# FFN input products of an encoder block: four instead of three of eight K-tile pairs by Strassen's scheme, with part of the sums formed by an accumulating DMA

## The chip, the cores and the metric

One core of one Trainium2 chip runs the whole block as one program. The metric is the device time of one execution in microseconds (us). TensorE (PE) multiplies, VectorE (DVE) and ScalarE (ACT) work elementwise, GpSimd (POOL) and SyncE (SP) here mostly issue DMAs; each engine takes its instructions in order from a queue of its own.

## The reference, cut to what matters

One layer, 256 tokens of width 2048, float32: a first FFN, a mixer of two attentions, a cross attention, a second FFN. The change lies in the two FFNs alone (`D_FF` is 5504):

```
def swiglu_ffn(x, w_in, w_out):
    g, u = jnp.split(x @ w_in, 2, axis=-1)
    return (jax.nn.silu(g) * u) @ w_out
h = layer_norm(ALPHA * h + 0.5 * swiglu_ffn(h, ffn1_w_in, ffn1_w_out), ...)
...
h = layer_norm(ALPHA * h + 0.5 * swiglu_ffn(h, ffn2_w_in, ffn2_w_out), ...)
```

## The kernel before

**Split products.** Each float32 operand is split into `hi` (a cast on ACT) and `lo = value - hi` (a subtraction on DVE); a product is three matmuls: hi·hi, lo·hi, hi·lo. All weights are streamed once, mostly 1 MB at a time, by SP into one of three `raw` buffers, then split into units of 128x1024 (four `hi` and four `lo` buffers).

**FFN input.** The 5504 columns of gate and of up are done in groups `j` of 512 columns (`j` = 0 to 9, and a narrow group 10). In a group the K dimension (2048) is walked in eight *items*, each a pair of K tiles (1 MB of weights: for each of the two K tiles, 512 columns of up and 512 of gate). An item done plainly (`mm_pair`, L296) is 2 K tiles x 2 token halves x 2 (gate, up) x 3 = 24 matmuls into four PSUM tiles. Group 0 is built apart in each FFN (`start`, `first_group`); groups 1 to 9 of both FFNs, 18 in all, go through `in_group`.

**Strassen items.** A pair of K tiles, two token halves and two column blocks is a 2x2 by 2x2 block product. For the items in `SUMS_AT` = (2, 4, 6) it is done with seven block products (`mm_sums`, L340), 7 x 3 = 21 matmuls. This needs sums of weight blocks. `form_sums` makes them on DVE in the buffer t (tag H5): one add of 1024 columns and two of 512 (L183). The two halves of t are then split (ACT L244, DVE L245) into two blocks, called here A (read by matmuls 10 to 15 of the item) and B (by matmuls 16 to 21); their buffers rotate over the tags X2, X3 and H4. It also needs sums of x, the forms (`sum_forms`, L311 and L315), made once per FFN for each of the Strassen items. After the last Strassen item of a group, `shared` combines four more PSUM tiles (L569 to L574) and `hidden` adds them and applies SiLU (L616 to L619).

**Turn and output.** The product of a group is transposed on PE eight times (L631) and split into H0 to H3: the *turn*, which is woven into the work after it, ahead of item 2 of the next group. After 12, then 16, then 15 K tiles (`F_SPLIT`) the output product (`out_proj`, L285) runs over what has been turned; there the last turn stands ahead of the third weight group.

**Order.** `run` walks the items, keeps loads and splits about one to two items ahead (`UNITS` = 4), and forms the sums of a Strassen item one item ahead. A scheduler then orders each engine's queue by priorities and by what is ready in its own reckoning; so neighbours in the code need not be neighbours in a queue.

Of the kernel before, what the change touches and what calls it, by code (L numbers as in the profile page):

```python
# [13 lines left out]
ALU = mybir.AluOpType  # L14
# [8 lines left out]
NF = D_FF // P  # L23
NG = D_FF // 512
F_SPLIT = (12, 16, 15)
SUMS_AT = (2, 4, 6)
SUM_TAGS = ("X2", "X3", "H4")
A_HEADS, A_DIM = 16, 64
B_HEADS, NOPE, ROPE, V_DIM = 16, 128, 64, 128
X_HEADS, X_DIM = 4, 512  # L30
# [44 lines left out]
class Sums:  # L75
# [1 line left out]

    def __init__(self, ap):  # L80
        self.ap = ap


class Kernel:
# [75 lines left out]
    def run(self):  # L160
        queue = [w if isinstance(w, (tuple, Sums)) else (w, None) for _, ws, _, _ in self.items for w in ws]
        ready, nxt, live = [], 0, 0

        def slots(w):
            if isinstance(w, Sums):
                return 2
            return 0 if w[1] else -(-w[0].shape[1] // 1024)

        raws, sums = {}, {}

        def fetch(i):
            if i not in raws:
                ap = queue[i].ap if isinstance(queue[i], Sums) else queue[i][0]
                raws[i] = self.raw_tile()
                self.last_load = self.nc.sync.dma_start(raws[i][:, :ap.shape[1]], ap)
            return raws[i]

        def form_sums(i):
            raw, t = fetch(i), self.block("H5", (P, 2048))
            for a, b, c in ((slice(0, 1024), raw[:, 0:1024], raw[:, 512:1536]),  # L180
                            (slice(1024, 1536), t[:, 0:512], raw[:, 1024:1536]),
                            (slice(1536, 2048), t[:, 1024:1536], raw[:, 1536:2048])):
                self.nc.vector.tensor_tensor(t[:, a], b, c, ALU.add)  # L183
            sums[i] = []
            for k in range(2):
                blk = self.block(SUM_TAGS[self.turns % len(SUM_TAGS)], (P, 2, 1024), F32R)
                self.turns += 1
                self.split(t[:, k * 1024:(k + 1) * 1024], blk[:, 0, :], blk[:, 1, :])
                sums[i].append((blk[:, 0, :], blk[:, 1, :]))

        def load(i):
            w = queue[i]
            raw = fetch(i)

            for k in (i, i + 1):
                if k < len(queue) and isinstance(queue[k], Sums) and k not in sums:
                    form_sums(k)
            got = []
            if isinstance(w, Sums):
                for a, b in ((1024, 2048), (0, 512)):  # L200
                    hi, lo = self.unit()
                    self.split(raw[:, a:b], hi[:, :b - a], lo[:, :b - a])
                    got.append((hi, lo))
                return got + sums[i]
            ap, tags = w
            n = ap.shape[1]
            if tags:
                blk = [self.block(g, (P, 2048), F32R) for g in tags[:2]]
            step = 768 if ap.tensor.name.endswith("_w_in_r") else 1024
            for c in range(0, n, step):  # L210
                m = min(step, n - c)
                hi, lo = [x[:, c:c + step] for x in blk] if tags else self.unit()
                self.nc.scalar.copy(hi[:, :m], raw[:, c:c + m])  # L213

                with self.tc.issue_after(self.chain.ins) if self.chain is not None else nullcontext():
                    self.nc.vector.tensor_tensor(lo[:, :m], raw[:, c:c + m], hi[:, :m].bitcast(F32), ALU.subtract)  # L216
# [12 lines left out]

        done = 0  # L230
        for fn, ws, held, prio in self.items:
            need = done + len(ws)
            while nxt < len(queue) and ahead(need, held):
                live += slots(queue[nxt])
                ready.append(load(nxt))
                nxt += 1
            units = [u for _ in ws for u in ready.pop(0)]
            live -= sum(slots(queue[done + i]) for i in range(len(ws)))
            done = need
            with self.prio(prio):  # L240
                fn(units) if ws else fn()
# [215 lines left out]
    def start(self):  # L457
# [4 lines left out]
        for _ in range(WARM):  # L462
            nc.tensor.matmul(warm[:, :P], self.ones, self.ones, start=True, stop=True)
        ps = self.group_tiles(0)
        xr = self.block("H0", (P, KT // 2, S)), self.block("H1", (P, KT // 2, S))
        for k in range(KT // 2):
            v = xr[k // 4][:, k % 4 * 2:k % 4 * 2 + 2, :]
            raw = self.raw_tile()
# [32 lines left out]
    def ffn(self, tag, xT, st, first=None, steps=None, late=None, before=None, tags=None):  # L501
# [4 lines left out]
        for half, nf in enumerate(F_SPLIT):  # L506
            hid = Act([])
            end = half == len(F_SPLIT) - 1
            for g in range(-(-nf // 4)):
# [11 lines left out]
                self.weave(main, {2: [turn]} if turn else {}, prio=0)  # L521
                hidden, turn = self.hidden(ps, j, g, n, hid, qs)
                self.add(hidden, prio=SOON)
                if j == 0:
                    self.add(lambda: setattr(self, "forms", self.sum_forms(xT())))
            if end and late:
                self.add(late)
            main = self.collect(
                self.out_proj, tag + "_w_out", f0, nf, lambda hid=hid: hid, half == 0,
                st if end else None, steps if end else None, tags)  # L530
            self.weave(main, {2: [turn]}, prio=0)
            turn = None
            f0 += nf

# [6 lines left out]
    def in_group(self, tag, j, n, xT, qs):  # L541
# [3 lines left out]
        for k in range(KT // 2):  # L545
            ap = src[:, k * 4 * n:(k + 1) * 4 * n]
            if n == 512 and k in SUMS_AT:
                i = SUMS_AT.index(k)

                def fn(w, i=i):  # L550
                    if i == 0:
                        qs.update((a, self.group_tile(j + 1)) for a in range(4))
                    self.mm_sums(ps, qs, w, xT(), self.forms, i)
                self.add(fn, Sums(ap))
# [22 lines left out]
    def first_group(self, tag, xT, before):  # L577
# [5 lines left out]
        def part(tt, g, tags=None, held=0, keep=False, again=False):  # L583
# [10 lines left out]
        first = self.collect(lambda: self.skewed(  # L594
            part, (), (None, None, ("X0", "X1", "early"), ("H4", "H5"))))
        self.weave(first, dict(zip((0, 2, 3), before)))
        for g in range(4):
            def fn(w, g=g):
                for tt in range(2):
# [36 lines left out]
    def out_proj(self, wname, k0, nk, x, scale, st, steps=None, tags=None):  # L636

# [22 lines left out]
        def part(n, tts, i, ps, tags=None, held=0, keep=False, again=False):  # L660
            grp = groups[i]

            def fn(w=None):
                if keep:
                    kept[i] = w
                w = kept.pop(i) if again else w
                for tt in tts:
                    if i == 0:
                        ps[tt] = self.mm_tile()
                    self.mm_tok(ps[tt], tt, w, x(), grp, i == 0, i == len(groups) - 1)  # L670
                if i == len(groups) - 1:
                    for tt in tts:
                        finish(tt, n, ps[tt])
# [2 lines left out]
            self.add(fn, *(() if again else ((ap, tags),)), held=held)  # L676

        last = len(groups) - 4
        for n in range(4):
            ps = {}  # L680
            for i in range(len(groups) if n < 3 or steps is None else last):
# [642 lines left out]
```

## Time and profile before

| | |
|---|---|
| median of 3 runs | 2531.34 us (2530.32 to 2535.32) |
| the profiled execution | 2533.1 us, of which the span is 2531.1 us |
| mean granted TensorE clock | 0.997 |
| busy: PE, DVE, ACT, POOL | 99%, 71%, 50%, 1% of the span |
| DMA | 488 MB, mean 193 GB/s, 52% of the 16 DMA engines on SP's queue, 2.0% on POOL's |

Busy PE is not PE at its peak, since matmuls overlap: one lasts 0.39 us, but they follow each other faster. In a timeline row stand the start in us, the busy us, the engine, the line, the operation, its tiles, and in brackets the idle time before it with what ended it. In a row by windows stand for each engine the busy us and the number of instructions, then the granted clock, the DMA share and GB/s. A row of DMA issues ends in KB and in the median us from issue to landing.

### The profile page before, as it was taken

Reading aid. Unit: us, or ns where it says so; the run is one execution under the profiler, and the core shown is the slowest. Engines: PE = TensorE matmul, PEld = TensorE weight load, DVE = VectorE, ACT = ScalarE, POOL = GpSimd, SP = SyncE. Lnnn points to the kernel's source line nnn. Section 1 sums busy time; section 2 is a strip of 40 time slices with the busy share of each in tenths; the row PEclk is TensorE's granted clock in tenths of the full one; section 3 lists DMA queues with packets and bytes.
Section 4 is the critical chain, followed back from the end, with each engine's and each line's share of the span. In section 5 each row is a group of like instructions: output and inputs, shape, how many; then the busy total and the mean of one; then the engine's idle time right before and its main releaser. Section 6 shows DMA issues by size and latency. Waiting matters only on the chain.

```text
span 2531.1 us, 32072 instructions
## 1 busy us (share of the span) xinstructions
PE 2511.4 (99%) x12590; PEld 2125.1 (84%) x12590; DVE 1809.3 (71%) x2420; ACT 1278.0 (50%) x1734; POOL 29.7 (1%) x87
## 2 busy tenths in 40 slices
PE   9999999999999999999999999999999999999998
PEld 8888888889888888888888888888878888888896
DVE  6967985796676776656568784555878688758856
ACT  5545553554444555544445554454645455445543
POOL 0000000000000000000000000000000000000000
PEclk9999999999999999999999999999999999999999
DMA  7655555555655644455556565543655554555563
GB/s 259 243 184 183 213 190 196 200 199 185 231 188 187 198 146 142 150 192 183 191 194 260 186 216 197 186 164 136 218 182 198 180 204 183 204 195 200 183 234 132
DMA packets 74039, 488.04 MB, mean 193 GB/s; under 512 B 8608, under 2 KB 8864, under 8 KB 20768
## 3 DMA queue, kind: packets, MB, share of 16 engines
q1 hardware_dynamic: 69216, 468.18, 51.9%
q0 software_dynamic: 3808, 15.73, 2.0%
q8 instruction: 98, 1.61, 0.3%
q10 hardware_dynamic: 864, 2.10, 0.2%
q14 instruction: 53, 0.43, 0.0%
HBM read 482.69 MB, written 2.10 MB: 192 GB/s over the span
## 4 chain that ended last, share of the span: by engine, by line
PE 94%; DVE 4%; DMA 2%; ACT 1%; issue 0%; DVEq 0%; ACTq 0%
PE mm L285 29%; PE mm L265 16%; PE mm L296 13%; PE at L296 10%; PE mm L266 8%; PE mm L340 5%; PE at L340 5%; PE mm L254 2%; DVE lo L216 1%; DMA raw<-ffn_w_out 1%; DMA raw<-ffn_w_in 1%; PE at L714 1%; PE at L1149 0%; PE at L1127 0%; PE at L862 0%
## 5 line engine op out<-in xcount | busy, mean ns | idle before, releaser
L216 DVE TENSOR_TENSOR lo<-raw,hi 128x1024 fp32r<-128x1024 f32 (+1 forms) x742 | 893.0, 1207 | 574.7 <-ACT hi L213 560.6
L213 ACT CAST hi<-raw 128x1024 fp32r<-128x1024 f32 (+1 forms) x742 | 769.7, 1039 | 912.2 <-PE mm L285 365.6
L285 PE MATMUL mm<-hi,H 128*128 128x512 f32 x1640 | 509.0, 390 | 1.9 <-ACT H L244 1.6
L265 PE MATMUL mm<-T,hi 128*128 128x512 f32 x1168 | 412.1, 396 | 0.0
L285 PEld LDWEIGHTS mm<-hi,H 128*128 128x128 f32 x1640 | 307.7, 188 | 66.8 <-ACT H L244 2.4
L266 PE MATMUL mm<-T,lo 128*128 128x256 f32 x1168 | 327.8, 281 | 0.0
L285 PE MATMUL mm<-lo,H 128*128 128x512 f32 x820 | 319.3, 389 | 0.1
L296 PE MATMUL mm<-hi,T 128*128 128x512 f32 (+1 forms) x1024 | 308.5, 376 | 0.1
L265 PEld LDWEIGHTS mm<-T,hi 128*128 128x128 f32 x1168 | 219.1, 188 | 51.5 <-issue 1.0
L296 PE MATMUL at<-hi,T 128*128 128x512 f32 x800 | 254.1, 391 | 0.0
L265 PE MATMUL mm<-H,hi 128*128 128x512 f32 x640 | 223.3, 393 | 0.0
L266 PEld LDWEIGHTS mm<-T,lo 128*128 128x128 f32 x1168 | 220.6, 189 | 0.1
L296 PEld LDWEIGHTS mm<-hi,T 128*128 128x128 f32 x1024 | 190.4, 188 | 30.8 <-ACT hi L244 1.0
L296 PE MATMUL mm<-lo,T 128*128 128x512 f32 (+1 forms) x512 | 193.1, 377 | 0.2 <-DVE lo L245 0.2
L285 PEld LDWEIGHTS mm<-lo,H 128*128 128x128 f32 x820 | 154.0, 188 | 32.3 <-DVE lo L216 0.7
L266 PE MATMUL mm<-H,lo 128*128 128x256 f32 x640 | 178.6, 279 | 0.0
L296 PEld LDWEIGHTS at<-hi,T 128*128 128x128 f32 x800 | 151.1, 189 | 31.5
L296 PE MATMUL at<-lo,T 128*128 128x512 f32 x400 | 156.6, 392 | 0.0
L265 PEld LDWEIGHTS mm<-H,hi 128*128 128x128 f32 x640 | 119.8, 187 | 26.7
L285 PE MATMUL mm<-hi,X 128*128 128x512 f32 x416 | 130.1, 390 | 0.0
L245 DVE TENSOR_TENSOR lo<-raw,hi 128x1024 fp32r<-128x1024 f32 (+1 forms) x126 | 119.1, 973 | 9.7 <-ACT hi L244 9.5
L244 ACT CAST hi<-raw 128x1024 fp32r<-128x1024 f32 (+1 forms) x126 | 103.6, 852 | 41.7 <-PE mm L296 12.4
(242 smaller groups left out, 3183.9 us busy)
## 6 DMA issues: line engine op xcount, KB each, us to landing
raw<-ffn_w_in SPq DMA_DIRECT2D x151, 1024.0 KB, 4.6
raw<-ffn_w_out SPq DMA_DIRECT2D x80, 1024.0 KB, 4.7
raw<-w_gate SPq DMA_DIRECT2D x32, 1024.0 KB, 4.8
raw<-w_qk SPq DMA_DIRECT2D x16, 1024.0 KB, 4.9
raw<-w_o_b SPq DMA_DIRECT2D x16, 1024.0 KB, 4.8
raw<-w_out SPq DMA_DIRECT2D x16, 1024.0 KB, 4.8
raw<-w_xk SPq DMA_DIRECT2D x16, 1024.0 KB, 5.0
raw<-w_xv SPq DMA_DIRECT2D x16, 1024.0 KB, 4.8
```

Of the source, the lines that this page charges most:

```text
L213: self.nc.scalar.copy(hi[:, :m], raw[:, c:c + m])
L216: self.nc.vector.tensor_tensor(lo[:, :m], raw[:, c:c + m], hi[:, :m].bitcast(F32), ALU.subtract)
L244: self.nc.scalar.copy(hi, src)
L245: self.nc.vector.tensor_tensor(lo, src, hi.bitcast(F32), ALU.subtract)
L254: self.nc.tensor.matmul(ps, w[u][wi][:, c:c + P], x.at(xi, kt), start=(j == 0 and k == 0), stop=(j == n - 1 and k == 2),)
L265: self.nc.tensor.matmul(ps, hi, x.both(kt), start=(kt == 0), stop=False)
L266: self.last_mm = self.nc.tensor.matmul(ps[:, :S], lo, x.at(0, kt), start=False, stop=(kt == n - 1))
L285: self.last_mm = self.nc.tensor.matmul(ps, x.at(xi, kt)[:, tt * P:(tt + 1) * P], w[u][wi][:, c:c + 512], start=(start and j == 0 and k == ...
L296: self.last_mm = self.nc.tensor.matmul(ps[tt, g][:, :n], x.at(xi, kt)[:, tt * P:(tt + 1) * P], hi_lo[wi][:, g * n:(g + 1) * n], start=(kt ...
L340: self.last_mm = self.nc.tensor.matmul(bank, a[xi], hi_lo[wi][:, c:c + 512], start=own and first and j == 0, stop=own and last and j == 2)
L714: self.nc.tensor.transpose(ps[:, i * P:(i + 1) * P], s[:, c:c + P], self.ident)
```

## The change

1. `SUMS_AT` becomes (2, 3, 5, 6): items 3 and 5 become Strassen items, item 4 a plain one; four of eight instead of three. The forms of x are made for four.
2. For the first three of them (`SUMS_DMA` = 3) the 1024-column sum is no longer DVE's: POOL's queue loads 512 KB of weights into t, and a second POOL DMA adds another 512 KB into it (`accum_op`), each begun up to three items ahead by `begin_sums`. SP then loads only 768 KB of that item, as two DMAs. The fourth Strassen item keeps the DVE sum.
3. t alternates between H4 and H5; the blocks A and B have X2 and X3 alone, so each Strassen item reuses the two buffers of the Strassen item before it.
4. The forms of x for the second FFN are made before the up half of group 0 instead of after its product. In `start`, x is staged in H4 and H5 instead of H0 and H1.
5. In `out_proj` the turn is called inside a weight group: for the 12-tile part between the two token halves of the second group, else ahead of the third group as before.

```diff
-SUMS_AT = (2, 4, 6)
-SUM_TAGS = ("X2", "X3", "H4")
+SUMS_AT = (2, 3, 5, 6)
+SUMS_DMA = 3
+SUM_TAGS = ("X2", "X3")
+ADD_TAGS = ("H4", "H5")
...
-                self.last_load = self.nc.sync.dma_start(raws[i][:, :ap.shape[1]], ap)
+                cols = ((0, 512), (1024, 2048)) if isinstance(w, Sums) and w.dma else ((0, ap.shape[1]),)
+                for a, b in cols:
+                    self.last_load = self.nc.sync.dma_start(raws[i][:, a:b], ap[:, a:b])
...
+        def begin_sums(i):
+            w = queue[i]
+            t = adds[i] = self.block(ADD_TAGS[len(adds) % 2], (P, 2048))
+            if w.dma:
+                self.nc.gpsimd.dma_start(t[:, :1024], w.ap[:, :1024])
+                self.nc.gpsimd.dma_start(t[:, :1024], w.ap[:, 512:1536], accum_op=ALU.add)
+
         def form_sums(i):
-            raw, t = fetch(i), self.block("H5", (P, 2048))
-            for a, b, c in ((slice(0, 1024), raw[:, 0:1024], raw[:, 512:1536]),
-                            (slice(1024, 1536), t[:, 0:512], raw[:, 1024:1536]),
-                            (slice(1536, 2048), t[:, 1024:1536], raw[:, 1536:2048])):
-                self.nc.vector.tensor_tensor(t[:, a], b, c, ALU.add)
+            raw, t = fetch(i), adds[i]
+            if not queue[i].dma:
+                self.nc.vector.tensor_tensor(t[:, :1024], raw[:, :1024], raw[:, 512:1536], ALU.add)
+            for k in range(2):
+                a = slice(1024 + 512 * k, 1536 + 512 * k)
+                self.nc.vector.tensor_tensor(t[:, a], t[:, 1024 * k:1024 * k + 512], raw[:, a], ALU.add)
...
+            for k in range(i, min(i + 4, len(queue))):
+                if isinstance(queue[k], Sums) and k not in adds:
+                    begin_sums(k)
...
-        xr = self.block("H0", (P, KT // 2, S)), self.block("H1", (P, KT // 2, S))
+        xr = self.block("H4", (P, KT // 2, S)), self.block("H5", (P, KT // 2, S))
...
-                if j == 0:
+                if j == 0 and not before:
                     self.add(lambda: setattr(self, "forms", self.sum_forms(xT())))
...
-            self.weave(main, {2: [turn]}, prio=0)
+            self.out_proj(tag + "_w_out", f0, nf, lambda hid=hid: hid, half == 0,
+                          st if end else None, steps if end else None, tags, turn)
...
         self.weave(first, dict(zip((0, 2, 3), before)))
+        self.add(lambda: setattr(self, "forms", self.sum_forms(xT())), prio=NEAR)
...
+                    if turn and (n, i, tt) == turn_at:
+                        turn()
...
+        turn_at = (0, 1, 1) if len(groups) == 3 else (0, 2, 0)
```

How this moves instructions is seen in the queues. In the changed kernel's lines, L196 and L193 are the adds of `form_sums` (512 and 1024 columns), L261 and L232 the splits (L245 and L216 before), L301 is `mm_tok` (L285 before), L646 the turn (L631 before).

DVE, first FFN, group 5, from the splits of the turn (H1) on. Before, items 2, 3, 4 are Strassen, plain, Strassen: the splits of A and B of item 4 (H4 and X2) read the t in H5 that DVE summed just ahead of them.

```order
L245 TENSOR_TENSOR H1_418_2342<-mm_419_2343,H1_418_2342 128x4x128
L183 TENSOR_TENSOR H5_411_2324<-raw_410_2322 128x1024
L245 TENSOR_TENSOR H1_418_2342<-mm_420_2350,H1_418_2342 128x4x128
L183 TENSOR_TENSOR H5_411_2324<-H5_411_2324,raw_410_2322 128x512
L245 TENSOR_TENSOR H4_412_2328<-H5_411_2324,H4_412_2328 128x1024
L183 TENSOR_TENSOR H5_411_2324<-H5_411_2324,raw_410_2322 128x512
L245 TENSOR_TENSOR lo_426_2383<-raw_410_2322,hi_425_2382 128x1024
```

The same place in the changed kernel: X2 and X3 from H5 are A and B of item 3, raw_440 is item 4, and the two L196 rows are item 5's adds, whose t (H4_420) POOL's two DMAs fill.

```order
L261 TENSOR_TENSOR H1_433_2409<-mm_435_2417,H1_433_2409 128x4x128
L232 TENSOR_TENSOR lo_445_2463<-raw_440_2449,hi_444_2462 128x1024
L196 TENSOR_TENSOR H4_420_2354<-H4_420_2354,raw_441_2451 128x512
L232 TENSOR_TENSOR lo_447_2467<-raw_440_2449,hi_446_2466 128x1024
L261 TENSOR_TENSOR X2_422_2362<-H5_399_2252,X2_422_2362 128x1024
L261 TENSOR_TENSOR X3_423_2365<-H5_399_2252,X3_423_2365 128x1024
L196 TENSOR_TENSOR H4_420_2354<-H4_420_2354,raw_441_2451 128x512
L193 TENSOR_TENSOR H5_428_2400<-raw_448_2491 128x1024
```

What moved: the first add of item 5, which waits for POOL's DMAs, stands ahead of the splits that item 3 needs. It stands so in 11 of the 18 groups (4, 5, 6, 8, 9 of the first FFN; 2, 4, 5, 6, 8, 9 of the second).

DVE, the same group, at its start, where the SiLU product of group 4 ends (L619) and item 2's splits follow. Before, the first `lo` of item 1 (raw_392) stands between the splits of A and B (X2, X3):

```order
L617 TENSOR_TENSOR w2_390_2198<-w2_390_2198,mm_339_1928 128x512
L183 TENSOR_TENSOR H5_394_2234<-H5_394_2234,raw_393_2232 128x512
L619 SCALAR_TENSOR_TENSOR w2_391_2199<-w2_390_2198,w2_391_2199 128x512
L183 TENSOR_TENSOR H5_394_2234<-H5_394_2234,raw_393_2232 128x512
L245 TENSOR_TENSOR X2_395_2238<-H5_394_2234,X2_395_2238 128x1024
L216 TENSOR_TENSOR lo_398_2245<-raw_392_2230,hi_397_2244 128x1024
L245 TENSOR_TENSOR X3_396_2241<-H5_394_2234,X3_396_2241 128x1024
```

In the changed kernel (raw_408 is item 1):

```order
L634 SCALAR_TENSOR_TENSOR w2_405_2264<-w2_404_2263,w2_405_2264 128x512
L196 TENSOR_TENSOR H4_393_2218<-H4_393_2218,raw_409_2299 128x512
L634 SCALAR_TENSOR_TENSOR w2_407_2266<-w2_406_2265,w2_407_2266 128x512
L261 TENSOR_TENSOR X2_410_2304<-H4_393_2218,X2_410_2304 128x1024
L261 TENSOR_TENSOR X3_411_2307<-H4_393_2218,X3_411_2307 128x1024
L232 TENSOR_TENSOR lo_413_2311<-raw_408_2297,hi_412_2310 128x1024
```

What moved: the first `lo` of item 1 is now behind both splits; and the split into X3 is the last reader of H4, into which POOL's next pair of DMAs (item 5's) then goes.

PE, first FFN, 12-tile part of `out_proj`, first quarter of the columns (mm_201, mm_202 before are the two token halves). Before, the turn stands right ahead of the first matmul that reads what it makes (H2):

```order
L285 MATMUL mm_202_1169<-lo_200_1145,H1_158_916 128x512
L285 MATMUL mm_202_1169<-hi_199_1144,H1_158_916 128x512
L631 MATMUL mm_214_1227<-ident_93,w2_193_1105 128x128 x4
L631 MATMUL mm_215_1234<-ident_93,w2_195_1107 128x128 x4
L285 MATMUL mm_201_1156<-hi_204_1184,H2_213_1226 128x512
```

In the changed kernel (mm_209, mm_210 are the two halves):

```order
L301 MATMUL mm_209_1191<-lo_208_1180,H1_164_944 128x512
L301 MATMUL mm_209_1191<-hi_207_1179,H1_164_944 128x512
L646 MATMUL mm_217_1240<-ident_93,w2_201_1140 128x128 x4
L646 MATMUL mm_218_1247<-ident_93,w2_203_1142 128x128 x4
L301 MATMUL mm_210_1204<-hi_205_1175,H1_164_944 128x512
```

What moved: between the transposes and the first reader of H2 now stand the 12 matmuls of the second token half (mm_210) of the group before.

More of the change, by code (lines that the diff above doesn't have):

```diff
@@ L75, with __init__ @@
 class Sums:
-    def __init__(self, ap):
-        self.ap = ap
+    def __init__(self, ap, dma):
+        self.ap, self.dma = ap, dma
 class Kernel:
@@ L167, in slots @@
             return 0 if w[1] else -(-w[0].shape[1] // 1024)
-        raws, sums = {}, {}
+        raws, sums, adds = {}, {}, {}
         def fetch(i):
             if i not in raws:
-                ap = queue[i].ap if isinstance(queue[i], Sums) else queue[i][0]
+                w = queue[i]
+                ap = w.ap if isinstance(w, Sums) else w[0]
                 raws[i] = self.raw_tile()
-                self.last_load = self.nc.sync.dma_start(raws[i][:, :ap.shape[1]], ap)
+                cols = ((0, 512), (1024, 2048)) if isinstance(w, Sums) and w.dma else ((0, ap.shape[1]),)
+                for a, b in cols:
+                    self.last_load = self.nc.sync.dma_start(raws[i][:, a:b], ap[:, a:b])
             return raws[i]
-        def form_sums(i):
-            raw, t = fetch(i), self.block("H5", (P, 2048))
-            for a, b, c in ((slice(0, 1024), raw[:, 0:1024], raw[:, 512:1536]),
-                            (slice(1024, 1536), t[:, 0:512], raw[:, 1024:1536]),
-                            (slice(1536, 2048), t[:, 1024:1536], raw[:, 1536:2048])):
-                self.nc.vector.tensor_tensor(t[:, a], b, c, ALU.add)
+        def begin_sums(i):
+            w = queue[i]
+            t = adds[i] = self.block(ADD_TAGS[len(adds) % 2], (P, 2048))
+            if w.dma:
+                self.nc.gpsimd.dma_start(t[:, :1024], w.ap[:, :1024])
+                self.nc.gpsimd.dma_start(t[:, :1024], w.ap[:, 512:1536], accum_op=ALU.add)
+        def form_sums(i):
+            raw, t = fetch(i), adds[i]
[4 more added lines that the diff above has]
+                self.nc.vector.tensor_tensor(t[:, a], t[:, 1024 * k:1024 * k + 512], raw[:, a], ALU.add)
             sums[i] = []
@@ L527, in ffn @@
                 self.add(late)
-            main = self.collect(
-                self.out_proj, tag + "_w_out", f0, nf, lambda hid=hid: hid, half == 0,
-                st if end else None, steps if end else None, tags)
-            self.weave(main, {2: [turn]}, prio=0)
+            self.out_proj(tag + "_w_out", f0, nf, lambda hid=hid: hid, half == 0,
+                          st if end else None, steps if end else None, tags, turn)
             turn = None
@@ L553, in fn @@
                     self.mm_sums(ps, qs, w, xT(), self.forms, i)
-                self.add(fn, Sums(ap))
+                self.add(fn, Sums(ap, i < SUMS_DMA))
                 if i == len(SUMS_AT) - 1:
@@ L634, in hidden, with out_proj @@
         return product, turn
-    def out_proj(self, wname, k0, nk, x, scale, st, steps=None, tags=None):
+    def out_proj(self, wname, k0, nk, x, scale, st, steps=None, tags=None, turn=None):
         nc, t, h = self.nc, self.t, self.h
```

## The prediction

> **What bounds the kernel.** I read the page's busy shares and its chain of waits first, then the chain inside one group.
>
> ```profile
> span 2531.1 us, 32072 instructions
> PE 2511.4 (99%) x12590; PEld 2125.1 (84%) x12590; DVE 1809.3 (71%) x2420; ACT 1278.0 (50%) x1734; POOL 29.7 (1%) x87
> PE 94%; DVE 4%; DMA 2%; ACT 1%; issue 0%; DVEq 0%; ACTq 0%
> ```
>
> PE is the bound: 94% of the chain that ended last. The chain in group 5 of the first FFN (start, us, what) gives PE's pace:
>
> ```profile
> 305.22 5.45 PE at L296 x24
> 310.67 1.36 PE at L340 x6
> 312.03 2.72 PE mm L340 x12
> 314.75 0.68 PE at L340 x3
> 315.43 5.44 PE at L296 x24
> ```
>
> A plain item is 24 matmuls in 5.44 us, 0.2267 us each; a Strassen item (the three middle rows, 21 matmuls) takes 4.76. So an item that becomes Strassen is worth 0.68 us, if PE never waits. Whether it waits is up to DVE, which in the whole of that group is nearly full:
>
> ```profile
> 288.44:331.07 42.63, 42.63 (x192) 35.06 (x192) 38.28 (x44) 24.18 (x29) 0.00 (x0) 1.00 0.54 197
> ```
>
> PE is busy for all of the 42.63 us, DVE for 38.28 (90%), ACT for 24.18; the clock is full, DMA at 0.54. DVE's pace is in its rows at the start of that group (288.44):
>
> ```profile
> 287.23 0.68 DVE L616 TENSOR_TENSOR w<-w,mm 128x512 f32<-128x512 f32 x1
> 288.48 0.69 DVE L616 TENSOR_TENSOR w<-w,mm 128x512 f32<-128x512 f32 x1
> ...
> 291.49 0.68 DVE L183 TENSOR_TENSOR H<-H,raw 128x512 f32<-128x512 f32 x1
> 292.09 1.22 DVE L245 TENSOR_TENSOR X<-H,X 128x1024 fp32r<-128x1024 f32 x1
> 293.23 1.22 DVE L216 TENSOR_TENSOR lo<-raw,hi 128x1024 fp32r<-128x1024 f32 x1
> 294.36 1.22 DVE L245 TENSOR_TENSOR X<-H,X 128x1024 fp32r<-128x1024 f32 x1
> ```
>
> They follow each other after 0.60 us (512 columns: 291.49 to 292.09) and 1.14 us (1024: 292.09 to 293.23). The first row starts 1.21 us before the group.
>
> **Matmuls removed.** 18 groups x 3 matmuls x 0.2267 = 12.2 us, all on the path: **-12.2**.
>
> **DVE's work per group.** Before: 5 plain items x 2 x 1.14, 3 Strassen items x (one add of 1.14, two of 0.60, three splits of 1.14, one of 0.60), and 12 x 0.60 of product and turn: 11.4 + 19.1 + 7.2 = 37.7, near the 38.28 above. After: 4 plain items 9.1, three Strassen items without the 1024 add 15.7, one with it 6.4, and 7.2: 38.4, in a group that would last 42.63 - 0.68 = 41.95: 92%. So DVE's total isn't the bound, but its order now counts. ACT does 4 x 2 casts in place of 5 x 2 and one set of 3.5 more, about 1.5 us more on 24.18: hidden.
>
> **The first `lo` of item 1.** In the changed order DVE has from 1.21 us before the group seven instructions of 0.60 and three of 1.14 before this `lo` is done: -1.21 + 4.2 + 3.4 = 6.4, seen by PE at about 6.5. PE starts item 1 at 5.44 and puts four matmuls that need only `hi` ahead: the `lo` is wanted at 6.35. Late by 0.2 us (an estimate; between 0 and 0.5), in the 11 groups that have this order: **+2.2**.
>
> **POOL's DMAs and item 5's add.** This is the disputed term. Count from a group's start. A and B of item 2 are split by -1.21 + 4.2 + 2.3 = 5.3 us; then H4 is free, and POOL may issue item 5's load, and after its landing the accumulating DMA. The first add of item 5 waits for both, and behind it on DVE stand a `lo` of item 4 and the split of A of item 3. Item 2 starts at 10.88 + 0.94 (turn) = 11.82, item 3 at 16.58, and its 11th matmul wants the `lo` of A at 18.85. With 0.60 + 1.14 + 1.14 ahead of that, the add must begin by 15.95. So the two DMAs have 15.95 - 5.4 = 10.5 us. If they come later, PE waits by the excess, in each of the 11 groups. The trace has no accumulating DMA. The nearest rows (KB, us to landing):
>
> ```profile
> raw<-ffn_w_in SPq DMA_DIRECT2D x151, 1024.0 KB, 4.6
> raw<-ffn_w_in_r SPq DMA_DIRECT2D x16, 768.0 KB, 4.3
> raw<-w_nope SPq DMA_DIRECT2D x16, 512.0 KB, 3.3
> w<-gb POOLq DMA_DIRECT2D x24, 256.0 KB, 4.4
> T<-gb POOLq DMA_DIRECT2D x2, 1024.0 KB, 5.8
> H<-memT POOLq DMA_DIRECT2D x2, 1024.0 KB, 10.5
> ```
>
> The load of 512 KB on POOL's queue lies between 4.4 (256 KB) and 5.8 (1 MB): 4.9. The accumulating DMA costs at least as much, 4.9, if its reading of t is hidden; at most 10.5, the slowest POOL row. It reads 512 KB from HBM and 512 KB of t, so I take the 1 MB row, 5.8. With 0.2 for two handovers: 10.9, late by 0.4: 11 x 0.4 = **+4.4**. At 4.9 it would be in time: 0. At 10.5 it would be late by 5.1: +56. The DMAs of items 2 and 3 have 12 us and more by the same count and cost nothing; what hides them is the 8 us and more between the freeing of H4 or H5 and their adds.
>
> The Trainium skill says that an adding DMA runs at about half a copy's rate, since it needs two source reads (Collectives: The Full Stack, "Why ReduceScatter is half of AllGather"). No run here shows that yet. By it 512 KB cost like 1 MB, and the sum below stays -9.4; by the copy's price it would be -13.8.
>
> SP's side: 768 KB land in 4.3 us. Item 5's `raw` is freed by the last split of item 2, some 10.6 us into the group, so it lands at about 15, just in time for the same add. DMA share: 8 MB per group become 10.25 and, with t read again, 11.75, so 0.54 becomes 0.69 to 0.79. That leaves room on average, but the load of item 4, that of item 5 and the accumulating DMA overlap, and this is why I don't take the lower end.
>
> **The moved turn.** In the 12-tile part of each FFN:
>
> ```profile
> 147.36 1.03 PE L631 MATMUL mm<-ident,w 128*128 128x128 f32 x8
> 149.19 0.50 PE L285 MATMUL mm<-hi,H 128*128 128x512 f32 x1 [0.79 <-ACT H L244]
> ...
> 150.01 0.40 PE L285 MATMUL mm<-lo,H 128*128 128x512 f32 x1
> 150.56 0.73 PE L285 MATMUL mm<-hi,H 128*128 128x512 f32 x2 [0.16 <-DVE H L245]
> ```
>
> Eight transposes (0.94) and four matmuls (0.91) after 147.36 should be over at 149.21; the next matmul starts at 150.56: 1.35 us lost. The change puts 12 matmuls (2.72 us) there, more than the wait: 2 x 1.35 = **-2.7** (bounds 0 and -2.7).
>
> **First FFN, group 1.** DVE makes a form more here, and item 3 comes sooner than item 4 did.
>
> ```profile
> 47.13 1.22 DVE L216 TENSOR_TENSOR lo<-raw,hi 128x1024 fp32r<-128x1024 f32 x1 [1.49 <-ACT hi L213]
> 58.21 0.48 DVE L315 TENSOR_TENSOR w<-w 128x128 f32<-128x128 f32 x2
> 58.62 0.28 DVE L315 TENSOR_TENSOR w<-w,w 128x128 f32<-128x128 f32 x1
> 58.82 0.68 DVE L311 TENSOR_TENSOR w<-T 128x512 f32<-128x512 f32 x1
> ...
> 84.98 1.23 DVE L216 TENSOR_TENSOR lo<-raw,hi 128x1024 fp32r<-128x1024 f32 x1 [1.07 <-ACT hi L213]
> 62.96 0.47 PE L340 MATMUL at<-hi,T 128*128 128x512 f32 x1
> ```
>
> DVE has no gap from 47.13 to 84. In the changed queue 9 instructions of 1.14, 19 of 0.60 and 16 of 0.20 (58.62 to 58.82) lie from this point to the end of the split of A of item 3: 24.9 us, so 72.0. PE starts item 2 at 62.96 and wants it 4.76 + 2.27 later, at 70.0: **+2.0** (0 to 4).
>
> **Second FFN, group 1.** Here DVE waited for a load and PE for DVE (PEld is the weight load that goes with each matmul):
>
> ```profile
> 1871.27 1.23 DVE L183 TENSOR_TENSOR H<-raw 128x1024 f32<-128x1024 f32 x1 [3.21 <-DMA raw<-ffn_w_in]
> 1873.87 0.19 PEld L296 LDWEIGHTS at<-lo,T 128*128 128x128 f32 x1
> 1877.76 2.21 PEld L340 LDWEIGHTS mm<-X,X 128*128 128x128 f32 x6 [3.70 <-DVE H L245]
> 1883.78 0.19 PEld L296 LDWEIGHTS at<-hi,T 128*128 128x128 f32 x1
> 1876.50:1884.00 7.50, 6.24 (x15) 4.97 (x16) 5.98 (x7) 1.50 (x2) 0.00 (x0) 0.54 0.77 279
> ```
>
> After a wait of 3.7 us the granted clock was 0.54 for this stretch. From 1873.87 to 1883.78 stand 16 matmuls' loads, 3.63 us at full pace, in 9.91: 6.3 us lost. The forms now come earlier, but item 5's add stands here ahead of a `lo` of item 3 and waits for POOL's DMAs, with DVE behind. Bounds: 0 (the wait stays) and -6.3 (gone). Neither has a nearer row, so I take the middle: **-3.1**.
>
> Staging x in H4 and H5 at the start is free: those two are idle until group 1's sums.
>
> **Sum.** -12.2 + 2.2 + 4.4 - 2.7 + 2.0 - 3.1 = **-9.4 us**. The profiled execution took 2533.1 us (2.0 outside its span), 1.8 above the median of the three runs; against its own time that is 2523.7, against the median 2531.34 it is 2521.9, rounded to **2522.0 us**. About 0.2% (5.1 us) is what a measurement of this kernel can tell from no change.
>
> **Rivals.**
> - *POOL's DMAs are late by more* (slower). The place is item 5's add in the 11 groups. Without this term the sum is -13.8, so the gain is gone at 1.25 us late (the pair takes 11.75 us), and from 1.7 us late (12.2 us) the kernel is slower by over 0.2%. For it: the 10.5 us row, and the overlap with two loads. Against: the rows of 4.4 and 5.8. At 2.5 us late: -13.8 + 27.5, 2545 us; the waits stay under the 3.7 us at which the clock fell.
> - *The DMAs are in time*: -13.8, and with the wait in the second FFN gone too, -17.0: 2514 to 2518 us. For it: the 3.3 us row of 512 KB on SP; it needs a pair within 10.5 us.
> - *DVE becomes the bound; the change doesn't do what it says.* If the 4.35 us per group in which DVE waited for ACT (42.63 - 38.28) can't be used, a group lasts 38.4 + 4.35 = 42.75, and the 12.2 us are lost: -2.7 + 2.0 - 3.1, about 2528 us. Against: these waits come from PE freeing `hi` buffers, so they shrink when PE is ahead.
>
> **Chances.** My forecast (2518 to 2526) 0.4; in time 0.2; DVE the bound or late by 0.9 to 1.7 us (2526 to 2536) 0.2; late by more 0.2. That is faster 0.57 (the first two, less a little for their upper edge), within 0.2% 0.22, slower 0.21. The range 2512 to 2541 reaches from the best case to a pair 2.1 us late.
>
> **What would show it.** Right: groups 4, 5, 6 last 42.2 to 42.7 us with 188 matmuls and transposes; DVE waits at L196 for a POOL DMA by a few tenths; the gap after L646 in the 12-tile parts is gone; the accumulating rows read 5 to 6.5 us. Wrong: PE waits at L356 for the split of A by 1 us or more in 11 groups, or the group at the start of the second FFN still has a stretch at half clock.

## The result, and the profile after

The changed kernel takes 2636.18 us (median of 4 runs), the kernel before 2531.53 us on the same chip: 1.0414 of before, 95% interval 1.0402 to 1.0427, so **105 us slower** where 9 us less were forecast. The predicted range ended at 2541. Later runs were on other chips, on which the kernel before took 2531.8 to 2537.3 us; so they are compared by their ratio to it (0.001 is 2.5 us).

The page of the changed kernel: span, busy shares, chain by engine, POOL's queue, DMA issues.

```profile
span 2631.6 us, 32385 instructions
PE 2533.8 (96%) x12536; PEld 2132.3 (81%) x12536; DVE 1823.9 (69%) x2468; ACT 1309.8 (50%) x1772; POOL 106.7 (4%) x195
q0 software_dynamic: 19360, 72.36, 11.2%
PE 68%; DMA 14%; DVE 14%; issue 3%; ACT 1%; SPq 0%; POOL 0%; DVEq 0%; ACTq 0%; POOLq 0%
raw<-ffn_w_in SPq DMA_DIRECT2D x97, 1024.0 KB, 6.0
H<-ffn_w_in POOLq DMA_DIRECT2D x108, 512.0 KB, 6.6
raw<-ffn_w_in SPq DMA_DIRECT2D x54, 512.0 KB, 6.7
```

The 54 matmuls are gone (12590 to 12536), yet PE is busy for 22 us longer, and it is idle for 97.8 us of the span where it was for 19.7. PE's share of the chain fell from 94% to 68%; DMA's rose from 2% to 14%, DVE's from 4% to 14%. SP's 1 MB loads of `w_in` land after 6.0 us instead of 4.6, its 512 KB pieces after 6.7.

How these hang together is seen in the chain of waits of one group (start, us, what; rows in between left out):

```profile
247.95 1.15 DVE lo L232
249.11 0.33 SPq L180
249.49 8.60 DMA raw<-ffn_w_in
258.19 0.69 DVE H L196
258.88 0.60 DVE w L587
...
266.54 2.27 DVE lo L232 x2
...
271.07 0.69 DVE lo L261
271.78 0.33 SPq L180
272.16 7.68 DMA raw<-ffn_w_in
279.94 0.69 DVE H L196
280.63 1.14 DVE lo L232
281.76 1.15 DVE X L261
282.95 0.78 PE at L356
```

From 247.95 to 282.95, 35 us, PE isn't on the path at all. It is a closed loop: a split on DVE frees a raw buffer (there are three), SP loads into it for 7.7 to 8.6 us, the first add of a Strassen item (L196) waits for that at the head of DVE's queue, and behind it stand the product (L587 and on) and the splits that free the next raw buffer. The loop is passed twice in a group: at 258.19 for item 2, at 279.94 for item 5. PE feels both. Its timeline at these places, and the granted clock in the stretch that follows the second wait (third last number):

```profile
267.73 0.50 PE L312 MATMUL mm<-lo,T 128*128 128x512 f32 x1 [2.19 <-DVE lo L232]
282.95 3.69 PE L356 MATMUL at<-X,X 128*128 128x512 f32 x8 [2.40 <-DVE X L261]
```
```profile
283.00:286.41 3.41, 3.41 (x8) 2.73 (x9) 2.77 (x3) 0.93 (x1) 0.00 (x0) 0.50 0.69 279
```

After 2.40 us without work PE ran at half clock for 3.41 us. Three groups of the first FFN (from the first to the fourth turn of its 16-tile part), before and after:

```profile
252.00:384.40 132.40, 132.40 (x594) 108.92 (x593) 114.93 (x129) 72.09 (x83) 0.00 (x0) 1.00 0.55 203
```
```profile
272.40:417.10 144.70, 131.89 (x565) 106.71 (x564) 113.70 (x131) 77.08 (x89) 11.36 (x16) 0.96 0.73 230
```

12.3 us more in three groups, PE idle for 12.8 of the 144.7 us, the clock at 0.96 on average, the DMA share 0.73, inside the 0.69 to 0.79 that was forecast.

POOL's second DMA, which adds, from issue to landing (all 54):

```profile
L188 POOL DMA_DIRECT2D H<-ffn_w_in x54: 870/878/898, 27.7 to 2466.7; - x54
DMA to landing us min/median/max: 5.4/7.9/11.5
```

5.8 had been taken. By item the median is 10.2 us (item 2), 5.6 (item 3) and 7.9 (item 5), and by the packet records SP's queue moves 2.5, 0.2 and 1.8 MB (medians) in that time: the adding DMA takes longer where more is loaded beside it. From the first issue to the second landing a pair takes 14.3, 13.7 and 11.9 us. In the packet records the packets of 4 KB take 328 ns (median), those of the copy ahead of it 159 ns.

Who waited for these transfers (us in total, times, the longest):

```profile
DVE H L196 <- DMA raw<-ffn_w_in: 75.5, 29, 5.0
ACT X L260 <- DMA H<-ffn_w_in: 62.6, 17, 9.4
DVE H L196 <- DMA H<-ffn_w_in: 12.1, 2, 7.5
```

By item: DVE's first add waits 13 times for item 2's load (43.6 us in all), once for item 3's, and at item 5 in 17 of the 18 groups, 15 times for SP's load (30.8 us) and twice for the pair. ACT's cast of block A, which reads the pair's sum directly, waits for item 2's pair in 16 groups. PE waits at L312 for the first `lo` of item 1, which stands on DVE behind item 2's add and the product, for 2.2 to 3.0 us in 11 groups (31.1 us), and at L356 for A of item 3, which stands behind item 5's add, in 15 groups (19.7 us).

### The profile page after: what moved, and what is told of

It reads as the page before. It is cut to its first block, busy times and chain, and to the rows that moved or that the text cites. A ratio compares the mean times of both kernels' runs of the same rounds, so it can differ in the third digit from the quotient of the medians.

```text
span 2631.6 us, 32385 instructions
## 1 busy us (share of the span) xinstructions
PE 2533.8 (96%) x12536; PEld 2132.3 (81%) x12536; DVE 1823.9 (69%) x2468; ACT 1309.8 (50%) x1772; POOL 106.7 (4%) x195
## 4 chain that ended last, share of the span: by engine, by line
PE 68%; DMA 14%; DVE 14%; issue 3%; ACT 1%; SPq 0%; POOL 0%; DVEq 0%; ACTq 0%; POOLq 0%
PE mm L301 30%; PE mm L281 15%; DMA raw<-ffn_w_in 9%; PE mm L282 8%; DMA H<-ffn_w_in 4%; PE mm L312 4%; DVE lo L232 4%; PE at L312 3%; DVE X L261 3%; PE mm L270 2%; DVE H L196 2%; PE mm L356 2%; PE at L356 1%; DVE lo L261 1%; DVE w L631 1%
## 5 line engine op out<-in xcount | busy, mean ns | idle before, releaser
L232 DVE TENSOR_TENSOR lo<-raw,hi 128x1024 fp32r<-128x1024 f32 (+1 forms) x706 | 845.9, 1206 | 523.1 <-ACT hi L229 510.9
L229 ACT CAST hi<-raw 128x1024 fp32r<-128x1024 f32 (+1 forms) x706 | 727.9, 1038 | 714.8 <-PE mm L301 372.8
L301 PE MATMUL mm<-hi,H 128*128 128x512 f32 x1640 | 511.2, 391 | 7.4 <-DVE w L632 7.4
L301 PEld LDWEIGHTS mm<-hi,H 128*128 128x128 f32 x1640 | 309.5, 189 | 73.0 <-ACT hi L229 9.0
L301 PE MATMUL mm<-lo,H 128*128 128x512 f32 x820 | 320.5, 391 | 0.0
L312 PE MATMUL mm<-hi,T 128*128 128x512 f32 (+1 forms) x896 | 275.9, 383 | 6.5 <-ACT hi L260 4.3
L260 ACT CAST X<-H 128x1024 fp32r<-128x1024 f32 x144 | 151.6, 1054 | 151.7 <-DMA H<-ffn_w_in 62.6
L260 ACT CAST hi<-raw 128x1024 fp32r<-128x1024 f32 (+1 forms) x162 | 133.9, 847 | 186.3 <-PE at L312 89.3
L312 PE MATMUL at<-hi,T 128*128 128x512 f32 x640 | 207.1, 397 | 0.1
L312 PEld LDWEIGHTS mm<-hi,T 128*128 128x128 f32 x896 | 171.0, 193 | 35.8 <-ACT hi L260 5.3
L312 PE MATMUL mm<-lo,T 128*128 128x512 f32 (+1 forms) x448 | 174.3, 389 | 21.7 <-DVE lo L232 20.5
L261 DVE TENSOR_TENSOR X<-H,X 128x1024 fp32r<-128x1024 f32 x144 | 171.9, 1219 | 25.2 <-ACT X L260 24.9
L261 DVE TENSOR_TENSOR lo<-raw,hi 128x1024 fp32r<-128x1024 f32 (+1 forms) x162 | 153.1, 968 | 42.1 <-ACT hi L260 42.0
L301 PEld LDWEIGHTS mm<-lo,H 128*128 128x128 f32 x820 | 154.7, 189 | 32.1 <-DVE lo L232 0.2
L196 DVE TENSOR_TENSOR H<-H,raw 128x512 f32<-128x512 f32 x144 | 98.6, 685 | 87.6 <-DMA raw<-ffn_w_in 75.5
L312 PEld LDWEIGHTS at<-hi,T 128*128 128x128 f32 x640 | 123.5, 193 | 26.9 <-DVE w L588 0.8
```

The lines of the kernel that those rows point to most:

```text
L196: self.nc.vector.tensor_tensor(t[:, a], t[:, 1024 * k:1024 * k + 512], raw[:, a], ALU.add)
L260: self.nc.scalar.copy(hi, src)
L261: self.nc.vector.tensor_tensor(lo, src, hi.bitcast(F32), ALU.subtract)
L301: self.last_mm = self.nc.tensor.matmul(ps, x.at(xi, kt)[:, tt * P:(tt + 1) * P], w[u][wi][:, c:c + 512], start=(start and j == 0 and k == ...
L312: self.last_mm = self.nc.tensor.matmul(ps[tt, g][:, :n], x.at(xi, kt)[:, tt * P:(tt + 1) * P], hi_lo[wi][:, g * n:(g + 1) * n], start=(kt ...
```

## The experiments

**Theory A:** the pairs on POOL's queue and SP's loads share the DMA engines, so that the loads of Strassen items and the pairs themselves land late; DVE and ACT wait for them at the head of their queues, PE waits for DVE, and its clock falls. **Theory D:** four Strassen items need more of the two blocks and of DVE's order than there is, DMAs or not.

### All sums on DVE, and no wide sum

```diff
-SUMS_DMA = 3
+SUMS_DMA = 0
```

> All three wide sums go back to DVE (no DMA on POOL, SP loads whole 1 MB); the four Strassen items, two blocks X2/X3 and the moved parts stay. Theory A (the accumulating DMA shares the 16 DMA engines with SP's loads at half rate, the raw loads of items 2 and 5 land in 8 to 10 us instead of 4 to 5, DVE's in-order queue waits for them and PE stalls twice in a group): the loads land in about 4.6 us again, the waits of DVE for raw go, and the time falls by 80 us or more, to 2525 to 2555 (DVE's 3 added sums of some 1.2 us take its work of a group from 38.4 to about 42 us, PE's own figure, so some waits for lo stay). Theory D (four Strassen items need more of the two blocks, of DVE's order and of the unit buffers than there is, whatever the DMAs do): 2620 to 2660, PE still waits over 4 us in a group.

**0.9928 (0.9914 to 0.9943): the loss is gone, and the kernel is faster than before**; 2520.5 us against 2537.2. Its page:

```profile
span 2513.1 us, 32141 instructions
PE 2495.9 (99%) x12536; PEld 2114.6 (84%) x12536; DVE 1878.9 (75%) x2522; ACT 1308.1 (52%) x1772; POOL 29.7 (1%) x87
```
```profile
251.80:381.80 130.00, 130.00 (x585) 107.46 (x584) 125.82 (x143) 76.62 (x90) 0.00 (x0) 1.00 0.59 206
```

In the same three groups DVE is busy for 97% (125.82 of 130.00 us) and PE never waits in them. Theory D falls. The expected range (from 2525) began 5 us too high, since it let some waits for `lo` stay.

No wide sum (`fetch` loads 1 MB again, POOL's two DMAs and the add of 1024 columns are out):

```diff
-                self.nc.vector.tensor_tensor(t[:, a], t[:, 1024 * k:1024 * k + 512], raw[:, a], ALU.add)
+                self.nc.vector.tensor_tensor(t[:, a], raw[:, 512 * k:512 * k + 512], raw[:, a], ALU.add)
-                self.split(t[:, k * 1024:(k + 1) * 1024], blk[:, 0, :], blk[:, 1, :])
+                self.split((raw, t)[k][:, k * 1024:(k + 1) * 1024], blk[:, 0, :], blk[:, 1, :])
```

> No wide sum at all: block A is split straight from the raw tile and the 512-wide adds read the raw tile (the first sums of every Strassen item are left out of the result), so there is neither a DMA on POOL nor a 1024-wide add on DVE; four Strassen items, two blocks, splits and moved parts stay. It is the best that any faster way of making the wide sums can give. Theory A: 2505 to 2525, group of 42 to 43 us. Theory D: 2600 or more, as the blocks and the order are as in the changed kernel.

0.9943 (0.9929 to 0.9958). A wide sum that cost nothing would be no better than one on DVE: there was nothing to gain in this kernel by taking it from DVE.

### The adding, the split load, and a pair that nobody waits for

```diff
-                self.nc.gpsimd.dma_start(t[:, :1024], w.ap[:, 512:1536], accum_op=ALU.add)
+                self.nc.gpsimd.dma_start(t[:, :1024], w.ap[:, 512:1536])
```

> POOL's second DMA no longer adds: it copies the same 512 KB over the first (the addition of the second operand is left out of the sums). Issues, bytes and order stay. Theory A, with the adding itself as the cause (328 against 159 ns for a 4 KB packet): 512 KB take some 2.5 us less of the engines, the raw loads land in 5 to 6 us, and the time falls by half of the loss or more, to 2530 to 2580. Rival C (two more DMAs on a second queue, or their bytes, do the harm, adding or not): the time stays within 20 us of 2636. Theory D: 2630 to 2640.

1.0152 (1.0137 to 1.0167), 2576 us. Of the 4.86% between 1.0414 and 0.9928 the adding accounts for 2.6% (66 us); 2.2% are there with two plain copies. So rival C (two more DMAs or their bytes, adding or not) holds for a part and not for the whole.

```diff
-                cols = ((0, 512), (1024, 2048)) if isinstance(w, Sums) and w.dma else ((0, ap.shape[1]),)
+                cols = ((0, ap.shape[1]),)
```

> SP's load of the three Strassen items is one DMA of 1 MB again instead of 256 KB and 512 KB (the 256 KB that nobody reads are loaded too); POOL's pair stays. Theory A: the bytes rise by 256 KB an item, nothing else is relieved, 2636 to 2665. Rival C2 (the split load with its 2 KB and 4 KB packets and its two issues is what is slow): the load lands in 5 to 6 us and the time falls by 40 us or more, to 2600 or less. Theory D: 2630 to 2640.

1.0507 (1.0489 to 1.0524), 2668 us. The range was counted from 2636 on the first chip; there 1.0507 is 2660 us, within theory A's range. The split of the load is no cause; its 256 KB less are worth 24 us here, which fits theory A, where bytes count.

The next run is the kernel without wide sums, with the pair put back:

```diff
             t = adds[i] = self.block(ADD_TAGS[len(adds) % 2], (P, 2048))
+            if w.dma:
+                self.nc.gpsimd.dma_start(t[:, :1024], w.ap[:, :1024])
+                self.nc.gpsimd.dma_start(t[:, :1024], w.ap[:, 512:1536], accum_op=ALU.add)
```

> The kernel without wide sums (block A is split straight from the raw tile, the first sums of the Strassen items are left out of the result), and beside it POOL's pair of DMAs as in the changed kernel, copy and accumulate, paced by the same two tiles, into a half of the tile that nobody reads; SP loads whole 1 MB. It is the run with whole loads and the pair (2667) with the one difference that no instruction waits for the pair. Theory A (what hurts is SP's late raw loads): 2630 to 2670, PE's waits stay as they were. Rival B (what hurts is that the adds and casts wait for the pair itself): 2520 to 2535, the loads are late but within their cover. Both in part: between, and the share is read from where it falls.

1.0168 (1.0150 to 1.0185), 2579 us: both in part. Without the pair the same kernel had 0.9943, so 2.25% (57 us) is traffic that nobody waits for, felt through SP's loads, which land after 6.8 us (with the pair) instead of 4.9 (without):

```profile
raw<-ffn_w_in SPq DMA_DIRECT2D x151, 1024.0 KB, 6.8
```
```profile
raw<-ffn_w_in SPq DMA_DIRECT2D x151, 1024.0 KB, 4.9
```

From there to the 1.0507 with whole loads, 3.4% (86 us), it is waiting for the pair. These two shares are those of the kernel with whole loads.

### One pair at a time

The edit for item 5; for item 2 `SUMS_DMA` is 1, for item 3 it is `i == 1`:

```diff
-                self.add(fn, Sums(ap, i < SUMS_DMA))
+                self.add(fn, Sums(ap, i == 2))
```

> The changed kernel with the accumulating pair in item 2 of a group only; items 3, 5 and 6 make their wide sum on DVE. Theory A (the pairs take the DMA engines from SP's loads, and PE stalls where an add waits for one): the loss over the kernel with all sums on DVE (2520 where before is 2537) falls with the number of pairs but not in proportion, since only the late loads of item 2 and those beside it stall PE: 2530 to 2560. Rival F (each pair costs the same, whatever is beside it): 2520 plus a third of 114, 2558. Rival G (only the pairs of items 3 and 5, which stand close together, do harm): 2518 to 2525.

> The changed kernel with the pair in item 3 alone; items 2, 5 and 6 sum on DVE. Its tile comes free with item 6 of the group before and is asked for one item after item 2, so what stands behind it in the queues is the same but for the product of the group. If the place at the turn of the groups is what costs (item 2, 80 us): 2518 to 2535 here. If every pair is asked for too early: 2570 to 2600.

> The changed kernel with the pair in item 5 alone (the one that the prediction priced); items 2, 3 and 6 sum on DVE. With item 2 alone the pair took some 14 us and cost 80 us. If the pair of item 5 takes as long against the 10.5 us that the prediction gave it: late by 3 to 4 us in 18 groups, 2570 to 2600. If beside one pair only its accumulate lands in about 6 us, as the prediction priced it: 2518 to 2530.

Item 2 alone: 1.0254 (1.0238 to 1.0270). Item 3 alone: 0.9977 (0.9966 to 0.9987). Item 5 alone: 1.0396 (1.0380 to 1.0411). Over the kernel with all sums on DVE that is 3.3, 0.5 and 4.7%: item 5's pair by itself costs as much as the three together, so the losses overlap and don't add. The expectations for items 2 and 5 were too low by 42 and 32 us at their upper ends; item 3 came out as the one by place had it. Group 5's pair in the run with item 5 alone:

```profile
313.82 0.55 POOL L187 DMA_DIRECT2D H<-ffn_w_in  x1 [41.47 <-DVE X L261]
318.24 0.87 POOL L188 DMA_DIRECT2D H<-ffn_w_in  x1 [3.88 <-DMA H<-ffn_w_in]
327.22 0.69 DVE L196 TENSOR_TENSOR H<-H,raw 128x512 f32<-128x512 f32 x1 [4.24 <-DMA H<-ffn_w_in]
329.10 2.60 PE L356 MATMUL mm<-X,X 128*128 128x512 f32 x8 [3.86 <-DVE X L261]
```

From the release of the tile (a split on DVE) to the add it is 13.4 us, where 10.5 had been counted. Over the run DVE waits at L196 8 times for the pair and 9 times for SP's load, which starts at the same time, and PE as often, 17 times, 4.2 us on average (us in total, times, the longest):

```profile
DVE H L196 <- DMA H<-ffn_w_in: 49.3, 8, 8.6
DVE H L196 <- DMA raw<-ffn_w_in: 36.0, 9, 4.9
PE mm L356 <- DVE X L261: 44.8, 9, 6.9
PE at L356 <- DVE X L261: 27.3, 8, 4.3
```

The two come almost together: the pair lands 4.4 us after DVE is ready for the add (median of the 18 groups), and the load, when it is last, little later. That is 72 us of PE's waiting, and the clock of 0.983 instead of 0.998 is 38 us more of PE's busy time (2533.6 against 2495.9): 110 of the 117 us by which the two spans differ. For item 2 the pair starts when item 5 of the group before releases the tile (244.96); its sum is asked for early, since its cast and add stand in the queues of ACT and DVE ahead of the product of that group:

```profile
244.96 0.54 POOL L187 DMA_DIRECT2D H<-ffn_w_in  x1 [105.31 <-DVE X L261]
249.24 0.88 POOL L188 DMA_DIRECT2D H<-ffn_w_in  x1 [3.74 <-DMA H<-ffn_w_in]
260.02 1.05 ACT L260 CAST X<-H 128x1024 fp32r<-128x1024 f32 x1 [2.95 <-DMA H<-ffn_w_in]
261.78 0.69 DVE L196 TENSOR_TENSOR H<-H,raw 128x512 f32<-128x512 f32 x1 [2.86 <-DMA raw<-ffn_w_in]
```

### The same sums asked for later

```diff
-            for k in (i, i + 1):
+            for k in (i,):
```

> The changed kernel with the sums of an item formed when that item is loaded, not already with the item before it: the adds and casts that wait for the pair and for the raw load stand one item (about 5 us of PE) later in DVE's and ACT's queues. Theory A2 (the pair of item 2 takes some 14 us from the release of its tile, is asked for about 12 us before PE uses the item, and all that stands behind the waiting add or cast, the product of the group and the splits of the next items, is late with it): the waits shrink by up to 5 us each, the time falls by 40 to 100 us, to 2535 to 2595. Rival H (PE waits because the sums themselves are ready too late, not what is queued behind them): they are then later still, 2640 to 2700.

> The run with late-formed sums with all sums on DVE and no pair: the control for the order alone. If the later place of the sums in DVE's and ACT's queues costs nothing of itself: 2515 to 2525, as with early sums (2520 where before is 2537). If PE then waits for the sums: 2530 to 2560, and the run with the pairs and late sums has to be read against it.

With the pairs 1.0331 (1.0305 to 1.0357), with all sums on DVE 0.9938 (0.9923 to 0.9953). The order costs nothing of itself, but with the pairs it brings back 0.8% only: 2617 us, between the two expectations. Later sums release their tile and their raw buffer later as well, and the next pair starts from that release; in a closed loop a consumer that is moved back takes its producer with it. That this is the whole reason was not tried apart.

### A pair that starts earlier, and one that doesn't add

The pair stays in item 5 alone. In the first and third of these runs `own` is true for item 5, so that it sums in H5 and all others in H4; the third has no pair. The second keeps the rotating tiles and leaves `accum_op` out, as above.

```diff
-            t = adds[i] = self.block(ADD_TAGS[len(adds) % 2], (P, 2048))
+            t = adds[i] = self.block(ADD_TAGS[w.own], (P, 2048))
```

> The pair in item 5 alone, as in the run that took 2632, but its tile is H5, which no other item uses (items 2, 3 and 6 sum in H4): the pair waits for the split of item 5 of the group before, not for that of item 2, and so can start some 30 us earlier. Bytes, packets and the accumulating DMA stay. Theory A3 (the loss comes from the pair needing some 14 us where it has 10.5 between the release of its tile and its add): 2518 to 2535. Rival (the adding DMA's traffic itself is the loss, by making SP's loads late): 2590 to 2640.

> The pair in item 5 alone, in the rotating tiles, with a plain copy as its second DMA (the addition of the second operand is left out of that item's sums). The pair then lands in 9 to 10.5 us: 4.1 for the first, 0.5 and some 5 for the second. If the prediction's 10.5 us from release to add is the right bound: in time or late by under 1 us, 2515 to 2540. If the bound is lower: 2560 or more.

> The control for the tile of its own: all sums on DVE, items 2, 3 and 6 in H4 and item 5 in H5. The one tile for items 2 and 3 makes item 3's sum wait for item 2's splits, which stand ahead of it in DVE's queue anyway: 2513 to 2525. If the tile costs: 2530 or more, and the run with the pair in H5 is read against it.

The control: 0.9940 (0.9926 to 0.9955). With the pair and its own tile: **1.0058 (1.0041 to 1.0076)** instead of 1.0396. The adding DMA is no faster here (median 9.8 us from issue to landing, against 9.0 with the rotating tiles), but it starts some 30 us ahead. So 3.4 of the 4.6% hang on when the pair runs. It then lands before the add asks for it, and it also no longer runs beside the load of its own item, whose 512 KB piece lands after 3.8 us instead of 8.6 (rotating tiles first, then the tile of its own):

```profile
raw<-ffn_w_in SPq DMA_DIRECT2D x18, 512.0 KB, 8.6
```
```profile
raw<-ffn_w_in SPq DMA_DIRECT2D x18, 512.0 KB, 3.8
```

Which of the two counts for more was not tried apart. Of the loss 1.2% (30 us) stay, between the two expectations, and stand in PE's waits for `lo` (22 us at L312 and L301) with DVE's add L193 waiting for SP's loads 13 times (24 us). With the plain second copy and the rotating tiles it is 1.0219 (1.0198 to 1.0240), 2594 us: not the expected 2515 to 2540 but the other branch, a lower bound than 10.5 us. The pair does land earlier, 11.5 us after its first issue (median) instead of 13.3, yet above the 9 to 10.5 that had been expected; and SP's load of the same item is then last in 12 of 17 waits:

```profile
DVE H L196 <- DMA raw<-ffn_w_in: 35.1, 12, 4.5
DVE H L196 <- DMA H<-ffn_w_in: 21.2, 5, 7.2
```

### The moved parts alone

The kernel before with one moved part each, the edit of `out_proj` and its call, and that of `sum_forms`' place, as in the change's diff:

```diff
+                    if turn and (n, i, tt) == turn_at:
+                        turn()
```
```diff
-                if j == 0:
+                if j == 0 and not before:
```

> The kernel before with the moved 12-tile turn alone (inside the second quarter of the W_out block, ahead of the matmuls of the second token tile). The prediction's term: 2 x 1.35 us less, 0.999 of before (2 to 3 us). If the turn was covered anyway: 0.9995 to 1.0005. If it blocks PE at its new place: 1.001 to 1.003.

> The kernel before with the moved forms of x alone, in FFN2 (formed in the first group, while the gate's matmuls run, instead of after it). The prediction's term: 0 to 6.3 us less, 3.1 taken: 0.9975 to 1.0. If DVE or ACT wait longer for the forms in the first group than after it: 1.0 to 1.002.

The turn alone: 0.9981 (0.9972 to 0.9989), 4.8 us less (2.8 to 7.1) where 2.7 were forecast; in its profile PE's wait in group 1 of the second FFN is 1.8 us instead of 3.3 as well, so not all of it need be the turn. The forms alone: 1.0006 (0.9997 to 1.0015), no gain; PE still waits 3.04 us for the split in group 1 of the second FFN. In the run with all sums on DVE the longest wait of PE in that group is 0.17 us:

```profile
1882.83 0.50 PE L356 MATMUL at<-lo,T 128*128 128x512 f32 x1 [0.17 <-DVE lo L261]
```

The version that beats both kernels is the change with all sums on DVE: 0.9928 of before, and by the two ratios 0.953 of the changed kernel (0.9928 / 1.0414).

## Why the prediction was wrong

- **The matmuls removed (-12.2), DVE no bound, no loss by four items:** right. With the DMAs out of the way and DVE at 97%, PE never waits for more than 0.96 us in the FFNs.
- **POOL's DMAs and item 5's add (+4.4, range 0 to +56), with SP's load "just in time" and the DMAs of items 2 and 3 at nothing:** the step that failed. It priced one pair against one add, and let everything that runs beside it keep its time. The pair of item 5 came out near its price, in the changed kernel 11.9 us instead of 10.9 (median), and landed 0.3 us after DVE was ready for the add (median; 0.4 late was forecast). That is luck in part: the copy took 3.7 us where 4.9 was taken, the adding DMA 7.9 where 5.8 was taken from a row of a plain 1 MB load, and DVE itself was late there. What the sum lacked:
  1. SP's load of item 5, "just in time" at 4.3 us. The 512 KB pieces of such loads take 6.7 us (median), and the load, not the pair, is last in 15 of the 17 waits at item 5's add, which last 1.8 us each (median).
  2. "The DMAs of items 2 and 3 ... cost nothing": right for item 3 (alone it costs 12 us, though not nothing), wrong for item 2 (alone 83 us), through which PE waits longer than through item 5 (31.1 against 19.7 us in the changed kernel). The 12 us of cover were counted to the add (the same sentence has 8 us, less than the pair's own 10.9), and the pair takes 14.3. The cast on ACT, which the prediction left out, waits for the pair, and the add on DVE for the load; both stand ahead of the product of the group before, so their wait reaches PE at the first `lo` of item 1 in item 2's own group.
  3. The loop. Casts and adds that wait free the raw buffers later, so the next loads start later.
  4. A wait of some us is not only these, since the clock falls.

  The number of groups was nearly right: PE waits for A of item 3 by 1 us or more in 12, where 11 were counted. With item 5's pair alone it is another picture, 17 groups and 4.2 us each; there the pair takes 13.3 us (median), 2.4 over the price, and SP's load of the item is as late.
- **"The waits stay under the 3.7 us at which the clock fell":** wrong; 2.4 us were enough in the changed kernel. The bound was read from the one long wait that the trace of before had.
- **DMA share 0.69 to 0.79:** right (0.73), and no comfort. A mean share below 1 says nothing of how late a load gets that starts together with two others.
- **The first `lo` of item 1 (+2.2) and group 1 of the first FFN (+2.0):** too high where nothing else waits. In the changed kernel that `lo` is late in just the 11 groups that were counted, but by item 2's wait and not by the order alone. In the run with all sums on DVE the longest gap of PE in the FFNs is 0.96 us, in that group 1. **The turn (-2.7)** was about right or a little small (-2.8 to -7.1 measured). **Group 1 of the second FFN (-3.1):** without the pairs PE's long wait there is gone, so it came out near its better bound, but not through the forms alone; with the pairs DVE waited 7.5 us for item 5's there, as the prediction's text feared and its middle value did not price.
- The sum with POOL's term left out was -13.8, or -17.0 with the wait in the second FFN gone. 0.9928 is -18 us (-14 to -22). The rival "in time" gave the time that the change has once its DMAs are left out; the terms under it were not all right one by one, so the agreement is partly luck.
- The Trainium skill's half rate for an adding DMA (Collectives: The Full Stack, "Why ReduceScatter is half of AllGather") agrees with the packets, 328 against 159 ns. The prediction drew from it the price of the adding DMA alone, not what that DMA takes from the loads beside it.

## What to carry to other kernels

Work that a DMA takes from an engine which isn't the bound gained nothing here and cost 4.9%: measure first what the kernel would do if that work were free. Price a DMA by its landing time beside the loads that will run with it, from the release of its buffer to its first reader, and look at what stands behind that reader in its in-order queue. Where a buffer ring is short, a load that is some microseconds slower can close a loop of release, load and use, and then everything in it is on the path.

## What was not expected of the hardware

- **The adding DMA:** 328 ns for a packet of 4 KB against 159 for a copy, 0.88 us of POOL to issue it against 0.54, 9.0 us for 512 KB where SP's queue moved 2.0 MB beside it (item 5 alone) and 6.2 where it moved 0.5 MB (item 3 alone; all medians).
- **Two queues on the same engines:** POOL's three pairs in a group, 1 MB each, move the landing of SP's 1 MB loads from 4.9 to 6.8 us, and the load of item 5 from 3.8 to 8.6 us by when the pair runs. SP's packets themselves are no slower: those of 8 KB take 309 ns (median) beside the copy and beside the adding DMA alike. The Trainium skill says that each DMA engine goes round its queues packet by packet (DMA: Bandwidth & Descriptors, "Arbitration"). That would make SP's packets wait for the slower ones of the adding queue, which fits the landings; the waiting itself is in no record here.
- **The clock:** but for the one at the end of the program every half-clock stretch lasted 3.41 us or a multiple. Counted over the profiled execution of all 17 kernels, gaps of PE of 1.0 to 1.9 us were followed by one within 5 us in 5 of 77 cases, of 1.9 to 2.5 us in 27 of 43, of 2.5 us and more in 79 of 87. The Trainium skill puts the limit at gaps of over 3.4 us (TensorE: Matmul & The Clock Gate, "HAM oscillation — how this bites in real kernels"); here it is lower.
